# First norm of an encoder layer on one core: block 0 scaled per partition after its transposes, blocks 1 to 3 by rows, and the order of the start rewritten around it

## The chip, the core and the metric

The kernel runs on 1 core of one Trainium2 chip. The metric is the time of one execution in device microseconds. The kernel before has a median of 910.9 us over 3 runs (910.83 to 911.63). The engines are named as in the profile: PE is TensorE (its matmuls; PEld its weight loads), DVE is VectorE, ACT is ScalarE, POOL is GpSimd, SP is SyncE, which here issues most of the DMAs; ACTq and SPq are the queues from which ACT and SP issue DMAs.

## The reference, cut to what matters

One encoder layer on x of 512 tokens by 1024 features, f32. The change touches the first norm, the residual that is kept of it, and the first projections:

```
def layer_norm(x, g, b):
    mu = mean(x, -1); var = mean(square(x - mu), -1)
    return (x - mu) * rsqrt(var + 1e-5) * g + b

h = layer_norm(x, ln_in_g, ln_in_b)          # (512, 1024)
z = h @ w_in                                 # (512, 5376): q, k, v of two head groups
qa, ka, va, qb, kb, vb = split(z)            # rope on q and k, banded attention on both groups
...
h = layer_norm(ALPHA * h + mix, ln1_g, ln1_b)
```

Then come a cross attention over 256 memory rows and a convolutional gated feed-forward of width 2816, each with its own norm.

## The kernel before, in words

**Tiling.** The 512 tokens are four blocks of 128 rows. A matmul takes the normalised activations transposed (features on partitions, 8 tiles of 128, called k = 0 to 7), and each f32 operand as a sum of two fp32r parts, hi (a copy rounded by ACT) and lo (raw minus hi, by DVE). A product is then three matmuls for each k: hi by hi, lo by hi, hi by lo. So every weight tile costs one cast on ACT (line 136, or 278 and 423 in the first stage) and one subtraction on DVE (line 138, or 282 and 428).

**The first stage** (lines 374 to 520) is written out by hand. Within `manual_schedule` the order of PE, DVE and ACT instructions is the order of the code; other instructions (weight splits of the next stage) are put between them by the scheduler when the program is built. For each block b there are these steps:

- `stats(b)`: mean and variance on DVE (line 312), and rsqrt as a power on POOL (line 109).
- `gain(b)` (line 341): (x - mu) * g; `shift(b)` (line 348): times rsqrt plus bias. Both on DVE, two instructions of 128x512 each. Their g and b stand as rows on all partitions: PE spreads them with a matmul by ones (`ones_t`), the gain copied by ACT to SBUF (`gin`), the bias left in a PSUM tile (`bt`).
- `turn(b)` (line 355): 8 transposes on PE into the PSUM tiles t and o; `t_hi(b)` (ACT, line 362) and `t_lo(b)` (DVE, line 367) write the parts Thi and Tlo.
- `hh`, `lh`, `hl`: the 24 matmuls of block b that make v of the first dilated group (512 columns of w_in), summed in one PSUM bank, `vps[b]`.
- `spill(b)` (line 371): ACT scales h by ALPHA and stores it to DRAM, for the residual much later.

Matmuls by ones without a use, `busy(n)`, are put in at several places of PE's order.

**PSUM.** The tag g has two banks, handed out in turn; the tag s has two tiles of two banks. Before, the gain rows use both g banks, then `vps[0]` and `vps[1]` use them, and `vps[2]`, `vps[3]` are the two halves of an s tile. The next stage starts with the K projection and the Q projection (`chunk_fm`, line 602), each of 24 matmuls into a g bank, and so each waits until the g bank's last holder has been copied out.

**The copies of v.** ACT copies `vps[0]` and `vps[1]` to SBUF (line 497) ahead of block 3's matmuls in the code, and `vps[2]` and `vps[3]` (line 519) at the stage's end, behind the two sine activations (lines 515 and 517), which wait for a chain of DVE instructions on the positions (lines 507 to 516).

**Queues.** DMAs share eight completion semaphores in turn, and an issue waits until the semaphore's last DMA has landed. `raw` has three buffers: a weight's load is issued when the lo subtraction that read the buffer three loads earlier is done.

```
    def g_tile():
        return ps_tile("g", 2)
...
        vps = [g_tile(), g_tile()]
        two = s_tile()
        vps += [two[:, i, :] for i in range(2)]
...
        nc.scalar.activation(rsn, ang, AF.Sin, scale=cst[:, CS : CS + 1])
        nc.vector.scalar_tensor_tensor(kk, ang, -1.0, ang, ALU.mult, ALU.max)
        nc.scalar.activation(rc, kk, AF.Sin, scale=-1.0, bias=halfpi)
        for b in range(2, 4):
            nc.scalar.copy(vt[:, b, :], vps[b])
```

Of the kernel before, what the change touches and what calls it, by code (L numbers as in the profile page):

```python
# [9 lines left out]
F32 = mybir.dt.float32  # L10
# [7 lines left out]
P = 128  # L18
# [31 lines left out]

MEM_AT = (2, 0)
SEVEN = (5, 7, 9, 11, 13, 15, 17, 19)
WARM = (12, 3)
CI, CF, CS, CMA, CM1, CM3 = 0, 128, 129, 130, 514, 770
CW = 898

# [16 lines left out]
def hymba_layer(ctx: ExitStack, tc: tile.TileContext, A, cst_d, out):  # L73
# [121 lines left out]
    def ps_tile(tag, bufs, shape=None):  # L195
        return gpool.tile(shape or [P, 512], F32, tag=tag, bufs=bufs, name=tag)

    def g_tile():
        return ps_tile("g", 2)

    def s_tile():
        return ps_tile("s", 2, [P, 2, 512])
# [52 lines left out]
    gt = halves(gin)  # L255
    sbt = s_tile()
    bt = [sbt[:, n, :] for n in range(2)]
    wv0 = []

    def v_raw(i):  # L260
# [15 lines left out]
    def v_hi(i):  # L276
        for raw, hi, _ in v_parts(i):
            nc.scalar.copy(hi, raw)
# [13 lines left out]
    snk = cpool.tile([P, 8], F32, name="snk")  # L292
    nc.sync.dma_start(snk, A["attn_sink"].partition_broadcast(P)[:, 0, :])
    nsnk = cpool.tile([P, 8], F32, name="nsnk")
    cpool.tile([P, 40], F32, name="cfill")

    gwc, gdc = (p1.tile([P, 32], F32, name=n)[:, 0:NB] for n in ("gwc", "gdc"))
    gw4 = A["g_win"][0].rearrange("(s j d) -> s d j", s=2, d=HD)
# [10 lines left out]
    def stats(b):  # L309
        st = spool.tile([P, 2, 6], F32, tag="st", name="st")  # L310
        for i in range(2):
            nc.vector.bn_stats(st[:, i, :], h[b][:, i * 512 : (i + 1) * 512])  # L312
        mv, LN["rs", b] = moments(st)
        LN["mu", b] = mv[:, 0:1]
# [35 lines left out]
    def turn(b):  # L350
        LN["T", b] = []
        for i in range(2):
# [4 lines left out]
                )  # L357
            LN["T", b].append(ps.rearrange("p (k t) -> p k t", k=4))

    def t_hi(b):  # L360
        for i, src in enumerate(LN["T", b]):
            nc.scalar.copy(hT[0][:, 4 * i : 4 * i + 4, b * P : (b + 1) * P], src)
# [11 lines left out]
    with tc.manual_schedule(engines={nc.tensor.engine, nc.vector.engine, nc.scalar.engine}):  # L374
        for v, name in enumerate(("ln_in_g", "ln_in_b")):
            nc.scalar.dma_start(rows[0:1, v].rearrange("p n f -> p (n f)"), A[name].partition_broadcast(1))
        nc.scalar.dma_start(cst[:, 0:CMA], cst_d[:, 0:CMA])
        spare = ps_tile("t", 1)

        def busy(n, ps=None):  # L380
            for _ in range(n):
                mm((spare if ps is None else ps)[:, 0:P], ones_t, ones_t, True, True)

        busy(WARM[0])
        gps = [g_tile(), g_tile()]
        for n in range(2):
            mm(gps[n], ones_t, rows[:, 0, n, :], True, True)
            nc.scalar.copy(gt[n], gps[n])
        for n in range(2):
            mm(bt[n], ones_t, rows[:, 1, n, :], True, True)  # L390
        busy(WARM[1])
        vps = [g_tile(), g_tile()]
        two = s_tile()
        vps += [two[:, i, :] for i in range(2)]
        count = [0] * NB

        def v_mm(b, ks, a, w):
            for k in ks:
                mm(
                    vps[b], hT[a][:, k, b * P : (b + 1) * P], wv0[k // 2][1][w][:, k % 2, :],  # L400
                    count[b] == 0, count[b] == 3 * KD - 1,
                )
                count[b] += 1

        def hh(b, *ks):
            v_mm(b, ks, 0, 0)

        def lh(b, *ks):
            v_mm(b, ks, 1, 0)

        def hl(b, *ks):
            v_mm(b, ks, 0, 1)

        all_k = range(KD)
        first = {}

        def w_raw(n, c0):
            first[n] = [wpool.tile([P, KD, P], F32, tag="raw", bufs=3, name="raw")]
            nc.sync.dma_start(first[n][0], w_in.rearrange("(k p) f -> p k f", p=P)[:, :, c0 : c0 + P])

        def w_hi(n):
            first[n].append(wpool.tile([P, KD, P], F32R, tag="hi", bufs=6, name="hi"))
            nc.scalar.copy(first[n][1], first[n][0])

        def w_lo(n):
            raw, hi = first[n]
            lo = wpool.tile([P, KD, P], F32R, tag="lo", bufs=6, name="lo")
            nc.vector.tensor_tensor(lo, raw, hi.bitcast(F32), ALU.subtract)
            first[n] = (hi, lo)

        stats(0)
        gain(0)
        shift(0)
        v_hi(0)
        turn(0)
        t_hi(0)
        stats(1)
        t_lo(0)
        v_hi(1)
        busy(3, vps[1])  # L440
        hh(0, 0, 1)
        busy(2, vps[1])
        lh(0, 0, 1)
        v_hi(2)
        hh(0, 2, 3)
        lh(0, 2, 3)
        v_hi(3)
        gain(1)
        shift(1)
        hh(0, 4, 5)  # L450
        lh(0, 4, 5)
        hh(0, 6, 7)
        turn(1)
        t_hi(1)
        lh(0, 6, 7)
        stats(2)
        sums(3, 0)
        t_lo(1)
        v_lo(0)
        w_raw("k", KB)  # L460
        hh(1, *all_k)
        lh(1, *all_k)
        neg_mean(3)
        sums(3, 1)
        v_lo(1)
        w_raw("q", QB)
        for b in range(2):
            hl(b, 0, 1, 2, 3)
        gain(2)
        shift(2)  # L470
        spill(0)
        turn(2)
        t_hi(2)
        v_lo(2)
        for b in range(2):
            hl(b, 4, 5)
        hh(2, *all_k)
        gain(3)
        root(3)
        t_lo(2)  # L480
        lh(2, *all_k)
        w_hi("k")
        v_lo(3)
        spill(1)
        shift(3)
        hl(2, 0, 1, 2, 3, 4, 5)
        turn(3)
        t_hi(3)
        w_lo("k")
        t_lo(3)  # L490
        nc.vector.tensor_scalar_mul(nsnk, snk, -1.0)
        for b in range(3):
            hl(b, 6, 7)
        w_hi("q")
        w_lo("q")
        for b in range(2):
            nc.scalar.copy(vt[:, b, :], vps[b])
        hh(3, *all_k)
        lh(3, *all_k)
        hl(3, *all_k)  # L500
        spill(2)

        rc, rsn = rope
        posi = zs[:, 0, :].bitcast(I32)
        nc.sync.dma_start(posi, A["positions"].partition_broadcast(P)[:, 0, :])
        ang = zs[:, 2, :]
        nc.vector.tensor_copy(ang, posi)
        nc.vector.tensor_scalar_mul(ang, ang, cst[:, CF : CF + 1])
        kk = zs[:, 1, :]
        nc.vector.tensor_scalar(kk, ang, 1.0 / TWO_PI, MAGIC, ALU.mult, ALU.add)  # L510
        nc.vector.tensor_scalar_add(kk, kk, -MAGIC)
        for cc in (C1, C2, C3):
            nc.vector.scalar_tensor_tensor(ang, kk, -cc, ang, ALU.mult, ALU.add)
        nc.vector.tensor_scalar(ang, ang, PI_IN, -PI_IN, ALU.min, ALU.max)
        nc.scalar.activation(rsn, ang, AF.Sin, scale=cst[:, CS : CS + 1])
        nc.vector.scalar_tensor_tensor(kk, ang, -1.0, ang, ALU.mult, ALU.max)
        nc.scalar.activation(rc, kk, AF.Sin, scale=-1.0, bias=halfpi)
        for b in range(2, 4):
            nc.scalar.copy(vt[:, b, :], vps[b])
        spill(3)  # L520

    SWAP = [(i + 8 if i < 8 else i - 8 if i < 16 else i) for i in range(32)]
    rn = [0]
# [1036 lines left out]
```

## Time and profile before

| | |
|---|---|
| median of 3 runs | 910.9 us (910.83 to 911.63) |
| the profiled execution's own time | 911.27 us |
| its span, first to last instruction | 909.5 us |
| PE busy | 896.6 us, 99% of the span |
| DVE, ACT, POOL busy | 62%, 42%, 14% |
| first useful matmul of v | 13.10 us from the span's start |
| first matmul of the K projection | 40.16 us |

A row of the timeline reads: start in us, duration in us, engine, line, operation, written tile `<-` read tiles, shapes, xN for N merged instructions, and in brackets how long the engine was idle before it and what ended that. A plain f32 matmul stands as two rows. "PEclk" or the column behind an interval's length is the clock that TensorE was granted, as a share of full speed.

### The profile page before, as it was taken

Reading aid. Unit: us, or ns where it says so; the run is one execution under the profiler, and the core shown is the slowest. Engines: PE = TensorE matmul, PEld = TensorE weight load, DVE = VectorE, ACT = ScalarE, POOL = GpSimd, SP = SyncE. Lnnn points to the kernel's source line nnn. Section 1 sums busy time; section 2 is a strip of 40 time slices with the busy share of each in tenths; the row PEclk is TensorE's granted clock in tenths of the full one; section 3 lists DMA queues with packets and bytes.
Section 4 is the critical chain, followed back from the end, with each engine's and each line's share of the span. In section 5 each row is a group of like instructions: output and inputs, shape, how many; then the busy total and the mean of one; then the engine's idle time right before and its main releaser. Section 6 shows DMA issues by size and latency. Waiting matters only on the chain.

```text
span 909.5 us, 12905 instructions
## 1 busy us (share of the span) xinstructions
PE 896.6 (99%) x5097; PEld 768.3 (84%) x5097; DVE 560.2 (62%) x956; ACT 385.0 (42%) x672; POOL 127.2 (14%) x106
## 2 busy tenths in 40 slices
PE   9999999999999999999999999999999999999996
PEld 7778987898878798788988889799999999888885
DVE  7975146335446667869466576877777767433346
ACT  4563436415545576315454224344444345222210
POOL 1064033431443420010000010000000000000001
PEclk9999999999999999999999999999999999999999
DMA  6762041214221337316222304233333354223201
GB/s 220 225 213 70 24 139 47 73 67 117 70 70 47 93 117 233 138 46 171 85 70 70 93 25 129 82 93 93 95 114 94 96 160 140 93 93 103 83 23 70
DMA packets 116942, 92.84 MB, mean 102 GB/s; under 512 B 12472, under 2 KB 100752, under 8 KB 116882
## 3 DMA queue, kind: packets, MB, share of 16 engines
q1 hardware_dynamic: 116048, 89.80, 32.4%
q10 hardware_dynamic: 834, 2.22, 0.6%
q8 instruction: 40, 0.66, 0.3%
q14 instruction: 20, 0.16, 0.1%
HBM read 87.82 MB, written 4.19 MB: 101 GB/s over the span
## 4 chain that ended last, share of the span: by engine, by line
PE 95%; DVE 3%; ACT 1%; DMA 1%; issue 0%; POOL 0%; DVEq 0%; ACTq 0%
PE g L168 54%; PE s L168 24%; PE o L168 5%; PE t L168 4%; PE o L694 3%; PE s L682 2%; PE s L208 1%; DMA vt<-in_ln_in_g_dram 1%; PE s L1225 0%; DVE lo L282 0%; DVE oA L348 0%; DVE st L312 0%; DVE Tlo L367 0%; POOL zs L530 0%; DVE mx L1206 0%
## 5 line engine op out<-in xcount | busy, mean ns | idle before, releaser
L138 DVE TENSOR_TENSOR lo<-raw,hi 128x1024 fp32r<-128x1024 f32 x126 | 157.2, 1249 | 86.6 <-ACT hi L136 85.9
L136 ACT CAST hi<-raw 128x1024 fp32r<-128x1024 f32 x126 | 132.3, 1051 | 141.5 <-PE g L168 92.5
L168 PE MATMUL g<-Thi,hi 128*128 128x512 f32 x240 | 94.8, 395 | 0.0
L168 PE MATMUL g<-Tlo,hi 128*128 128x512 f32 x240 | 94.2, 393 | 0.0
L168 PE MATMUL g<-Thi,lo 128*128 128x512 f32 x240 | 94.0, 392 | 0.0
L109 POOL TENSOR_TENSOR rs<-ve,mhalf 128x1 f32<-128x1 f32 x18 | 15.3, 852 | 524.9 <-DVE ve L115 513.6
L530 POOL TENSOR_TENSOR zs<-zs,rsn 128x512 f32<-128x512 f32 x29 | 59.2, 2040 | 147.5 <-DVE zs L529 147.5
L168 PE MATMUL g<-Uhi,hi 128*128 128x512 f32 (+1 forms) x224 | 77.5, 346 | 1.0 <-ACT hi L136 1.0
L168 PE MATMUL g<-Ulo,hi 128*128 128x512 f32 (+1 forms) x224 | 77.1, 344 | 0.0
L168 PE MATMUL g<-Uhi,lo 128*128 128x512 f32 (+1 forms) x224 | 77.0, 344 | 0.0
L168 PE MATMUL g<-hi,Thi 128*128 128x512 f32 x184 | 71.6, 399 | 0.0
L168 PE MATMUL g<-hi,Tlo 128*128 128x512 f32 x184 | 70.9, 395 | 0.5 <-DVE Tlo L1173 0.5
L168 PE MATMUL g<-lo,Thi 128*128 128x512 f32 x184 | 70.7, 395 | 0.4 <-DVE lo L282 0.4
L528 DVE TENSOR_TENSOR zs<-g,rc 128x512 f32<-128x512 f32 x29 | 20.0, 689 | 68.2 <-PE g L168 31.6
L168 PE MATMUL g<-x,hi 128*128 128x256 f32 x320 | 58.8, 284 | 0.0
L168 PEld LDWEIGHTS g<-Thi,hi 128*128 128x128 f32 x240 | 45.1, 188 | 11.1 <-issue 0.9
L168 PEld LDWEIGHTS g<-Tlo,hi 128*128 128x128 f32 x240 | 45.1, 188 | 10.3 <-issue 1.4
L168 PEld LDWEIGHTS g<-Thi,lo 128*128 128x128 f32 x240 | 45.1, 188 | 9.3
L168 PEld LDWEIGHTS g<-x,hi 128*128 128x128 f32 x320 | 50.0, 192 | 0.5 <-issue 0.3
L168 PEld LDWEIGHTS g<-hi,Tlo 128*128 128x128 f32 x184 | 42.2, 230 | 6.4 <-DVE Tlo L1173 1.0
L168 PEld LDWEIGHTS g<-Uhi,hi 128*128 128x128 f32 x224 | 42.5, 190 | 5.8 <-ACT hi L136 1.2
L138 DVE TENSOR_TENSOR lo<-act,hi 128x512 fp32r<-128x512 f32 x22 | 14.8, 690 | 52.8 <-ACT hi L136 52.8
(363 smaller groups left out, 2091.8 us busy)
## 6 DMA issues: line engine op xcount, KB each, us to landing
raw<-in_w_in_dram SPq DMA_DIRECT2D x37, 512.0 KB, 3.8
raw<-in_w_gate_dram SPq DMA_DIRECT2D x22, 512.0 KB, 3.8
raw<-in_w_up_dram SPq DMA_DIRECT2D x22, 512.0 KB, 3.9
raw<-in_w_down_dram SPq DMA_DIRECT2D x22, 512.0 KB, 3.4
raw<-in_w_xk_dram SPq DMA_DIRECT2D x8, 512.0 KB, 3.9
raw<-in_w_xv_dram SPq DMA_DIRECT2D x8, 512.0 KB, 3.5
raw<-in_w_xq_dram SPq DMA_DIRECT2D x8, 512.0 KB, 4.6
raw<-in_w_xo_dram SPq DMA_DIRECT2D x8, 512.0 KB, 3.5
```

The lines of the kernel that those rows point to most:

```text
L109: nc.gpsimd.tensor_tensor(out_, in_, mhalf, ALU.pow)
L136: nc.scalar.copy(hi, raw)
L138: (eng or nc.vector).tensor_tensor(lo, raw, hi.bitcast(F32), ALU.subtract)
L168: on_pe(nc.tensor.matmul(o, l, r, start=first, stop=last))
L208: on_pe(nc.tensor.transpose(ps[:, i // 4, f : f + P], t[:, i * P : (i + 1) * P], ident))
L528: nc.vector.tensor_tensor(zc, ps, rc, ALU.mult)
L530: nc.gpsimd.tensor_tensor(sh, sh, rsn, ALU.mult)
L682: nc.tensor.transpose(tp[:, k, :], s_, ident)
L694: nc.tensor.matmul(o[HJ[j], t0:t1], lhs(j), rhs(j), start=i == 0, stop=i == len(parts) - 1)
```

## The change

- **Block 0** no longer has `gain` and `shift`. One DVE instruction (x - mu) * rs over 128x1024 normalises the rows; these are transposed; then, with features on partitions, g and b are one number per partition. `col_scale` applies them from PSUM into a new tile `fp0` (two tiles of k on ACT, six on DVE), and `col_hi` and `col_lo` make Thi and Tlo from it.
- The numbers per partition come as follows: two further DMAs on ACT's queue bring g and b as 8 rows of 128 each (`grow`), PE transposes the 16 rows, and DVE copies the result to `gcol`.
- **Block 0's residual** is made of the normalised rows by `resid`, four DVE instructions of 128x512 in two places, in place of `spill(0)` on ACT. The other spills move up by one place each.
- `stats(1)` and `v_hi(0)` go ahead of the gain rows; the bias rows go behind block 0's transposes; all `busy` matmuls but the first 12 are gone.
- `vps` changes places: blocks 0 and 1 now have the halves of the s tile, blocks 2 and 3 the two g banks.

The diff, with what only moves a constant left out:

```
-WARM = (12, 3)
+WARM = (12,)
...
+    fp0 = wpool.tile([P, KD, P], F32, tag="gb", bufs=2, name="fp0")
+    gcol = cpool.tile([P, 2 * KD], F32, name="gcol")
+    grow = zs[0 : 2 * KD, 1, 0:P]
...
+    def col_scale(ks, eng):
+        for k in ks:
+            g, o, src = gcol[:, k : k + 1], gcol[:, KD + k : KD + k + 1], LN["T", 0][k // 4][:, k % 4, :]
+            if eng is nc.scalar:
+                nc.scalar.activation(fp0[:, k, :], src, AF.Identity, scale=g, bias=o)
+            else:
+                nc.vector.tensor_scalar(fp0[:, k, :], src, g, o, ALU.mult, ALU.add)
+    def col_hi(k0, k1):
+        nc.scalar.copy(hT[0][:, k0:k1, 0:P], fp0[:, k0:k1, :])
+    def col_lo(k0, k1):
+        nc.vector.tensor_tensor(hT[1][:, k0:k1, 0:P], fp0[:, k0:k1, :], hT[0][:, k0:k1, 0:P].bitcast(F32), ALU.subtract)
+    def resid(part):
+        ah = oW[:, 0:2, :]
+        for i, z in enumerate(halves(h[0])):
+            if part == 0:
+                nc.vector.scalar_tensor_tensor(ah[:, i, :], z, ALPHA, gt[i], ALU.mult, ALU.mult)
+            else:
+                nc.vector.scalar_tensor_tensor(ah[:, i, :], bt[i], ALPHA, ah[:, i, :], ALU.mult, ALU.add)
+        if part == 1:
+            nc.scalar.dma_start(h_dram[0:P, :], ah.rearrange("p a f -> p (a f)"))
...
+        for v, name in enumerate(("ln_in_g", "ln_in_b")):
+            nc.scalar.dma_start(grow[v * KD : (v + 1) * KD, :], A[name].rearrange("(k p) -> k p", p=P))
...
         busy(WARM[0])
+        stats(0)
+        nc.vector.tensor_scalar(h[0], h[0], LN["mu", 0], LN["rs", 0], ALU.subtract, ALU.mult)
+        stats(1)
+        v_hi(0)
         gps = [g_tile(), g_tile()]
         for n in range(2):
             mm(gps[n], ones_t, rows[:, 0, n, :], True, True)
             nc.scalar.copy(gt[n], gps[n])
+        two = s_tile()
+        nc.tensor.transpose(two[:, 1, 0 : 2 * KD], grow, ident[0 : 2 * KD, 0 : 2 * KD])
+        nc.vector.tensor_copy(gcol, two[:, 1, 0 : 2 * KD])
+        turn(0)
         for n in range(2):
             mm(bt[n], ones_t, rows[:, 1, n, :], True, True)
-        busy(WARM[1])
-        vps = [g_tile(), g_tile()]
-        two = s_tile()
-        vps += [two[:, i, :] for i in range(2)]
+        vps = [two[:, i, :] for i in range(2)] + [g_tile(), g_tile()]
...
-        stats(0)
-        gain(0)
-        shift(0)
-        v_hi(0)
-        turn(0)
-        t_hi(0)
-        stats(1)
-        t_lo(0)
+        col_scale((0, 1), nc.scalar)
+        col_scale(range(2, KD), nc.vector)
+        col_hi(0, 2)
+        col_hi(2, 4)
+        col_lo(0, 4)
         v_hi(1)
-        busy(3, vps[1])
         hh(0, 0, 1)
-        busy(2, vps[1])
         lh(0, 0, 1)
+        col_hi(4, 8)
+        gain(1)
+        col_lo(4, 8)
...
-        spill(0)
+        spill(1)
...
-        spill(1)
+        spill(2)
...
+        resid(0)
         t_lo(3)
...
         w_lo("q")
+        resid(1)
         for b in range(2):
             nc.scalar.copy(vt[:, b, :], vps[b])
...
-        spill(2)
+        spill(3)
...
         for b in range(2, 4):
             nc.scalar.copy(vt[:, b, :], vps[b])
-        spill(3)
```

**How the order moves: PE at the start.** Before, from the first matmuls by ones (t) over the gain rows (g), the bias rows (s) and block 0's transposes (L355) on; the waits for semaphores stand in brackets (DMAHW is a DMA's, Pool, DVE and Activation an engine's).

```order
L168 MATMUL t<-zs 128x128 x11
L168 MATMUL g<-vt,zs 128x512 [waits DMAHW3_49,DVE_49]
L168 MATMUL g<-vt,zs 128x512
L168 MATMUL s<-vt,zs 128x512 [waits DMAHW5_49,Pool_49]
L168 MATMUL s<-vt,zs 128x512
L168 MATMUL t<-zs 128x128 x3
L355 MATMUL t<-cst,oA 128x128 [waits DMAHW0_49,DMAHW7_49,DVE_49,PE_49]
```

And PE at the start now (L425 is the transpose of the 16 rows of `grow`, L358 those of block 0):

```order
L168 MATMUL t<-zs 128x128 x11
L168 MATMUL g<-vt,zs 128x512 [waits DMAHW3_49,DVE_49]
L168 MATMUL g<-vt,zs 128x512
L425 MATMUL s<-cst,zs 128x16 [waits DMAHW7_49,DMAHW3_49,DMAHW1_49]
L358 MATMUL t<-cst,oA 128x128 [waits DVE_49,PE_49]
L358 MATMUL t<-cst,oA 128x128 x3
L358 MATMUL o<-cst,oA 128x128 x4
L168 MATMUL s<-vt,zs 128x512 [waits DMAHW5_49,Pool_49]
```

Ahead of block 0's transposes there now stands one that waits for three DMAs, and the bias rows have moved behind them.

**ACT at the head of its new DMAs.** What ACT's queue now holds there; the second pair brings `grow`.

```order
L405 DMA vt<-in_ln_in_g_dram 1x1024 [waits DVE_49]
L405 DMA vt<-in_ln_in_b_dram 1x1024 [waits Pool_49]
L406 DMA cst<-in_constants_dram 128x130
L408 DMA zs<-in_ln_in_g_dram 8x128 [waits DMAHW1_49]
L408 DMA zs<-in_ln_in_b_dram 8x128 [waits DMAHW3_49]
```

Before, only the first three stood there; the new two wait for DMAs that were issued earlier on the same semaphores (the first weight tile and the gain row).

**ACT at the end of the first stage.** Before, from the copies of `vps[0]` and `vps[1]` (g banks) on:

```order
L497 COPY vt<-g 128x512 x2
L371 ACTIVATE oW<-oB 128x1024
L136 CAST hi<-raw 128x1024
L372 DMA h_dram<-oW 128x1024
L136 CAST hi<-raw 128x1024 x3
L515 ACT_TABLE_LOAD
L515 ACTIVATE rsn<-zs,cst 128x512
L517 ACTIVATE rc<-zs,halfpi 128x512
L519 COPY vt<-s 128x512 x2
```

The same place now:

```order
L532 COPY vt<-s 128x512 x2
L400 ACTIVATE oW<-oB 128x1024
L136 CAST hi<-raw 128x1024
L401 DMA h_dram<-oW 128x1024
L136 CAST hi<-raw 128x1024
L550 ACT_TABLE_LOAD
L550 ACTIVATE rsn<-zs,cst 128x512
L552 ACTIVATE rc<-zs,halfpi 128x512
L554 COPY vt<-g 128x512 x2
```

The copies that free the g banks have gone from ahead of the casts and the sines to behind them; those that free an s tile have gone the other way.

**DVE at the same place, now,** from the lo part of the Q weights on (zs is the chain on the positions, L138 the lo parts of the next four weight tiles, L385 the second half of `resid`):

```order
L464 TENSOR_TENSOR lo<-raw,hi 128x1024
L385 SCALAR_TENSOR_TENSOR oW<-s,oW 128x512 x2
L542 CAST zs<-zs 128x512
L543 TENSOR_SCALAR zs<-zs,cst 128x512
L138 TENSOR_TENSOR lo<-raw,hi 128x1024
L545 TENSOR_SCALAR zs<-zs 128x512
L138 TENSOR_TENSOR lo<-raw,hi 128x1024
L546 TENSOR_SCALAR zs<-zs 128x512
L548 SCALAR_TENSOR_TENSOR zs<-zs 128x512
L138 TENSOR_TENSOR lo<-raw,hi 128x1024
L548 SCALAR_TENSOR_TENSOR zs<-zs 128x512 x2
L138 TENSOR_TENSOR lo<-raw,hi 128x1024
```

Before, five of the zs instructions stood ahead of the first L138; now two do, and the last one (L551, L516 before) stands behind all four of them, where before it stood behind three.

More of the change, by code (lines that the diff above doesn't have):

```diff
@@ L294, in hymba_layer @@
     nsnk = cpool.tile([P, 8], F32, name="nsnk")
-    cpool.tile([P, 40], F32, name="cfill")
+    cpool.tile([P, 24], F32, name="cfill")
     gwc, gdc = (p1.tile([P, 32], F32, name=n)[:, 0:NB] for n in ("gwc", "gdc"))
@@ L429, in w_lo @@
             first[n] = (hi, lo)
-        stats(0)
-        gain(0)
-        shift(0)
-        v_hi(0)
-        turn(0)
-        t_hi(0)
-        stats(1)
-        t_lo(0)
+        col_scale((0, 1), nc.scalar)
[3 more added lines that the diff above has]
+        col_lo(0, 4)
         v_hi(1)
-        busy(3, vps[1])
         hh(0, 0, 1)
-        busy(2, vps[1])
         lh(0, 0, 1)
-        v_hi(2)
+        col_hi(4, 8)
+        gain(1)
+        col_lo(4, 8)
         hh(0, 2, 3)
         lh(0, 2, 3)
-        v_hi(3)
-        gain(1)
-        shift(1)
+        v_hi(2)
         hh(0, 4, 5)
         lh(0, 4, 5)
+        v_hi(3)
+        shift(1)
         hh(0, 6, 7)
+        lh(0, 6, 7)
         turn(1)
         t_hi(1)
-        lh(0, 6, 7)
         stats(2)
```

## The prediction

> **What bounds the kernel now.** I read the page's busy table first, then PE's waits behind the first stage, then the timeline of all engines from 30 to 48 us.
>
> ```profile
> span 909.5 us, 12905 instructions
> ...
> PE 896.6 (99%) x5097; PEld 768.3 (84%) x5097; DVE 560.2 (62%) x956; ACT 385.0 (42%) x672; POOL 127.2 (14%) x106
> ```
>
> PE is busy 99% of the span, so whatever makes PE stand still is paid in full, unless PE had a later wait that shrinks by it. The waits of PE between 41 us and the end, all of them:
>
> ```profile
> PE g L168 <- ACT hi L136: 1.0, 1, 1.0
> PE g L168 <- DVE Tlo L1173: 0.5, 1, 0.5
> PE s L168 <- POOL x L531: 0.3, 1, 0.3
> PE s L682 <- ACT pu L774: 0.3, 1, 0.3
> ```
>
> They come to 2.1 us. So a delay of PE at 40 us can be given back by at most 2.1 us later; the rest arrives at the end. The question is when PE finishes v of the four blocks, and when it starts on the K projection. The timeline there:
>
> ```profile
> 31.38 1.22 DVE L428 TENSOR_TENSOR lo<-raw,hi 128x1024 fp32r<-128x1024 f32 x1
> 33.71 0.69 DVE L367 TENSOR_TENSOR Tlo<-t,Thi 128x512 fp32r<-128x512 f32 x1 [1.11 <-ACT Thi L362]
> ...
> 35.00 1.09 ACT L497 COPY vt<-g 128x512 f32<-128x512 f32 x2
> 35.15 1.23 DVE L428 TENSOR_TENSOR lo<-raw,hi 128x1024 fp32r<-128x1024 f32 x1
> 36.40 1.00 SPq L626 DMA_DIRECT2D raw<-in_w_in_dram  x2
> 38.35 1.98 PE L168 MATMUL s<-lo,Thi 128*128 128x512 f32 x8
> 39.06 1.23 DVE L138 TENSOR_TENSOR lo<-raw,hi 128x1024 fp32r<-128x1024 f32 x1 [0.17 <-PE s L168]
> 40.16 0.39 PE L168 MATMUL g<-Thi,hi 128*128 128x512 f32 x1
> 40.31 2.10 SPq L146 DMA_DIRECT2D raw<-in_w_in_dram  x2
> 42.22 1.05 ACT L136 CAST hi<-raw 128x1024 fp32r<-128x1024 f32 x1 [3.03 <-DMA raw<-in_w_in_dram]
> 44.25 1.05 ACT L136 CAST hi<-raw 128x1024 fp32r<-128x1024 f32 x1 [0.97 <-DMA raw<-in_w_in_dram]
> 47.24 0.71 ACT L517 ACTIVATE rc<-zs,halfpi 128x512 f32<-128x512 f32 x1
> 47.86 1.05 ACT L519 COPY vt<-s 128x512 f32<-128x512 f32 x2
> ```
>
> The last eight matmuls of v (38.35) run at 1.81 / 8 = 0.226 us each, and K's first matmul (40.16) follows without a gap. Its g bank was block 0's; ACT had copied that out at 35.00. Blocks 2 and 3, in an s tile, are copied out only at 47.86: ACT first waits for two weight tiles (42.22 and 44.25, idle 3.03 and 0.97 ahead of them) and runs the sines. Before, nobody needs that s tile by then.
>
> **The change, first term: the K projection behind the sines.** Now blocks 2 and 3 hold the g banks, so K's first matmul needs the copy that stands behind the sines, and Q's the one after it. Nothing that waits on PE's order can fill the hole: PE takes its instructions in order. With the old times alone, K would start when the first of the two copies (1.05 / 2) is done, at 48.4: 8.2 us late.
>
> It comes later still, since DVE's work around it grows. I need DVE's short operations on the positions:
>
> ```profile
> 37.27 0.43 DVE L510 TENSOR_SCALAR zs<-zs 128x512 f32<-128x512 f32 x1
> ...
> 38.19 0.69 DVE L513 SCALAR_TENSOR_TENSOR zs<-zs 128x512 f32<-128x512 f32 x1
> ```
>
> `resid` adds four operations of the second kind: at a little under 0.69 each, 1.31 in each of its two places (of the pair at 14.71, below, the last ends after 1.41). The first stands behind the lo part of K's weights; DVE is idle 1.11 us there (row 33.71), so it costs what follows only 0.2 to 0.3, or all 1.31 if that idle time is used up by DVE's own delay. Let all of v be 0.6 us late (second term). Then t_lo(3) runs from about 34.5, the lo part of Q's weights ends at 37.1 (36.38 before), and the second half of `resid` and the first two operations on the positions end at 39.35. The first L138 needs PE's second pair among the last eight, 0.7 behind their start as before (39.06 to 38.35): 39.65 to 40.85.
>
> Two DMAs hang on this, by the three raw buffers. The one behind Q's lo part took 42.22 - 36.38 = 5.84 until ACT began on it: 42.95 now, and its cast ends at 44.0. The one behind the first L138 took 44.25 - 40.31 = 3.94: 44.8, cast until 45.85. DVE takes the third L138 44.05 to 45.2 (1.15 from start to start), two operations of 0.66 until 46.5, the fourth L138 until 47.65, then 0.45 and 0.69 for the last two of the positions: 48.75. The cosine takes 0.71, the copy another 0.57: K starts at about 50.1. That is 9.95 us late in all, 0.6 of it v's delay, so PE stands about 9.3 us. The shortest hole is the old time, 8.2 less the 0.2 between; the longest adds both halves of `resid` in full to it, 8.2 + 2.6 = 10.8.
>
> **Second term: the start.** Rows of the chain of waits and of the timeline:
>
> ```profile
> 1.96 4.69 DMA vt<-in_ln_in_g_dram
> 4.41 1.66 SPq L268 DMA_DIRECT2D raw<-in_w_in_dram  x2
> 8.58 1.88 PE L168 MATMUL s<-vt,zs 128*128 128x512 f32 x4
> 11.41 0.63 PE L355 MATMUL t<-cst,oA 128*128 128x128 f32 x4 [0.28 <-PE t L168]
> 13.10 0.71 PE L168 MATMUL g<-hi,Thi 128*128 128x512 f32 x2
> 14.71 1.41 DVE L341 SCALAR_TENSOR_TENSOR oA<-oA,mv,gin 128x512 f32<-128x512 f32 x2
> 17.34 1.28 DVE L312 BATCH_NORM_STATS2 st<-oB 128x6 f32<-128x512 f32 x2
> 59.10 0.29 DVE L725 CUSTOM_DVE_ANT_0 pu<-s,cst 128x128 f32<-128x128 f32 x1
> 59.43 0.40 ACT L728 ACTIVATE pu<-pu,stT 128x128 f32<-128x128 f32 x1 [0.63 <-DVE stT L725]
> ```
>
> The change takes away `gain(0)` and `shift(0)` and lets the statistics of blocks 0 and 1 run in idle time of DVE, but all of block 0 now waits for the two small DMAs of `grow`. ACT can't issue the second one before the gain row has landed: 1.96 + 4.69 = 6.65. (The first waits for the first weight tile, for which SP's second issue of line 268, ended at 6.07, waited too.) No row shows a DMA of 8 rows of 512 bytes on ACT's queue in this traffic. The nearest is the gain row itself, 4.69 from issue to landing; the ends are the fastest and the slowest medians of the DMA table that come into question:
>
> ```profile
> out_dram<-h SPq DMA_DIRECT2D x8, 256.0 KB, 2.1
> ...
> cst<-in_constants_dram ACTq DMA_DIRECT2D x1, 65.0 KB, 5.5
> ```
>
> I take 4.69: landed at 11.35 (8.75 to 12.15). The Trainium skill, page "DMA: Bandwidth & Descriptors", section "Anatomy of one DMA — SWDGE (gpsimd) path", gives a DMA about 2.0 us of fixed cost plus its bytes over 436 GB/s. By that rule `grow` would be there at about 8.7; the gain row's 4.69 for 4 KB speaks against it in this traffic.
>
> Behind the landing: transpose and `gcol` until 11.8; block 0's transposes 11.5 to 12.6 (0.63 for four); two scales on ACT (0.40, the second 0.3 later) until 12.7; six on DVE at 0.2 to 0.29 until 14.1; col_lo 0.6; `gain(1)` 1.31, col_lo 0.6, `shift(1)` 1.31. So stats(2) starts at 17.95, against 17.34: 0.6 late (2.0 early to 1.4 late with the bounds). From there DVE's list is the old one, and so v ends 0.6 late. PE's own start, 12.6 + 1.7 for the bias rows (8.58) = 14.3 against 13.10, is hidden behind DVE. ACT's table load and `v_hi(0)` come later too, but the gain rows are needed by DVE only at 14.7: nothing. The loads of x's blocks 2 and 3 are issued one landing later, 1.3 us; stats(2) has that to spare.
>
> **Third term: the clock.** The first matmuls, the same kind when warm, and the end of the span, with the granted clock third from the end in the last two rows:
>
> ```profile
> 0.99 4.97 PE L168 MATMUL t<-zs 128*128 128x128 f32 x24 [0.99 <-POOL zs L247]
> 12.52 0.83 PE L168 MATMUL g<-zs 128*128 128x128 f32 x6
> 901.57 0.39 PE L168 MATMUL g<-hi,lo 128*128 128x512 f32 x1
> 902.00:906.00 4.00, 0.00 (x0) 0.00 (x0) 3.90 (x8) 0.00 (x0) 0.92 (x1) 1.00 0.00 0
> 906.00:909.50 3.50, 0.00 (x0) 0.00 (x0) 0.48 (x1) 0.00 (x0) 0.00 (x0) 0.55 0.40 150
> ```
>
> After the last matmul (ended 901.96) the clock stays full past 906 and is about half from then on: some 4 us of standing still take it away. At the start, 24 matmuls took 0.207 each where later six took at most 0.14: half speed for 4 to 5 us of work. A hole of 9.3 us is over the 4 us, so K starts at half speed. For 4.5 us it does 10 matmuls in place of 20; 10 x 0.226 = 2.2 us lost (0 if the clock stays, 2.5 if it takes 4.97). The Trainium skill, page "TensorE: Matmul & The Clock Gate", section "What's actually happening", says the clock falls to half after an idle window of about 3.4 us and comes back after a busy one. By that figure the term would be 1.7 and the time 922.3; the trace agrees on the half.
>
> **Sum.** 9.95 for K's start, 2.2 for the clock, less 0.3 for the later wait on POOL, whose chain no longer starts late: 11.85 us. On the profiled execution's 911.27 (its span 909.5 and 1.77 around it) that is 923.1; on the median of 910.9, 0.4 lower, 922.8.
>
> **Rivals.**
> - `grow` lands early, at about 8.75: v ends 2.0 early in place of 0.6 late, the hole stays: 922.8 - 2.6 = 920.2. For it: 4 KB is little. Against: the gain row, as small, took 4.69. It is also what the Trainium skill's DMA page would give.
> - The clock isn't lost in the hole: 920.6. Against it stands the end of the span.
> - The clock is lost at the start as well. PE would stand from 8.6 to 11.4, 2.8 us, which is under 4; if `grow` comes at 12.15 it is 3.6. Then block 0's transposes, the bias rows and the first eight or so matmuls run at half, some 2.5 us more on top of 0.8: 926.
> - Not slower: K's bank is free earlier, because K's first matmul waits for the copy of block 0, not of block 2. Place: the two copies of v. Price: the hole of 9.3 and the clock's 2.2 go, 922.8 - 11.5 = 911.3, and with an early `grow` 908.7. It decides as soon as that copy ends before v does (40.9). The code hands out the two g banks in turn, and the last two holders are blocks 2 and 3, so this would need another bank for K than I read.
>
> **How the numbers follow.** Forecast 0.62; early `grow` 0.14; clock kept 0.07; clock lost twice 0.13; bank free 0.04, half of it with an early `grow`. About 0.2%, 1.8 us, is what a measurement can tell from no change; only the last rival gets within it (0.02) or below it (0.02), so slower has 0.96. The range goes from 919.0 (early `grow` with the shortest hole, 8.0 of 9.3) to 926.0 (clock lost twice).
>
> **What would show it.** In the changed kernel's profile: a wait of PE for ACT's copy at line 554, 8 to 11 us long, ahead of the first g<-Thi,hi; rows of K's first ten matmuls about 0.45 apart; a granted clock near half in those microseconds; the copy of vt<-g behind the cosine at about 50; L425 on PE at about 11.4. Wrong would be: K without a gap behind v, or a hole under 6 us, or PE's later waits shrinking by more than 2.

## The result and the profile after

The changed kernel takes 923.71 us (923.35 to 925.34, 4 runs), against 911.0 (910.83 to 911.63): 1.0141 times as long, 95% interval 1.0129 to 1.0153, or 12.7 us more. The profiled execution is the longest of the four, 925.34; the other three had spans of 921.5 to 922.0, so some 1.6 of what its rows add up to isn't in the median.

The page's busy table, and the waits of PE from 41 us to the end (total, times, longest), of the changed kernel:

```profile
span 923.5 us, 12890 instructions
...
PE 899.0 (97%) x5082; PEld 768.4 (83%) x5082; DVE 562.0 (61%) x964; ACT 385.1 (42%) x674; POOL 125.9 (14%) x106
```

```profile
PE g L168 <- ACT vt L554: 9.2, 1, 9.2
PE g L168 <- ACT hi L136: 1.0, 1, 1.0
PE s L716 <- ACT pu L808: 0.9, 2, 0.6
PE g L168 <- DVE Tlo L1207: 0.5, 1, 0.5
```

One wait is new, and it is the one that the first step named: the K projection waits for ACT's copy of block 2's bank. The later ones are those of before, but that POOL's 0.3 is gone and ACT's 0.3 for `pu` is 0.9. The timeline around the hole:

```profile
39.85 1.98 PE L168 MATMUL g<-lo,Thi 128*128 128x512 f32 x8
...
46.35 1.04 ACT L136 CAST hi<-raw 128x1024 fp32r<-128x1024 f32 x1 [2.81 <-DMA raw<-in_w_in_dram]
...
49.81 0.72 ACT L552 ACTIVATE rc<-zs,halfpi 128x512 f32<-128x512 f32 x1
50.44 1.05 ACT L554 COPY vt<-g 128x512 f32<-128x512 f32 x2
51.06 0.80 PE L168 MATMUL g<-Thi,hi 128*128 128x512 f32 x1 [9.23 <-ACT vt L554]
...
55.49 0.40 PE L168 MATMUL g<-Tlo,hi 128*128 128x512 f32 x1
```

The last eight matmuls of v start 1.5 later than before (38.35), PE stands 9.23, and K starts at 51.06, 10.9 late. Its first ten matmuls start 0.44 apart on average ((55.49 - 51.06) / 10); behind 55.49 it is 0.23 to 0.24. The same stretches by interval; the column behind POOL's is the granted clock:

```profile
8.60:10.90 2.30, 0.00 (x0) 0.00 (x0) 0.69 (x3) 1.51 (x3) 0.55 (x1) 1.00 1.14 392
11.10:12.90 1.80, 1.80 (x10) 1.80 (x10) 0.17 (x1) 0.66 (x2) 0.00 (x0) 0.51 0.88 310
13.00:14.50 1.50, 1.50 (x3) 0.52 (x2) 1.42 (x5) 1.11 (x4) 0.00 (x0) 0.50 1.00 372
...
41.90:45.20 3.30, 0.00 (x0) 0.00 (x0) 3.27 (x5) 1.65 (x2) 0.00 (x0) 1.00 0.83 257
45.30:51.00 5.70, 0.00 (x0) 0.00 (x0) 3.70 (x6) 4.24 (x6) 0.00 (x0) 0.50 0.97 316
51.10:55.50 4.40, 4.40 (x11) 3.43 (x12) 0.00 (x0) 0.39 (x1) 0.00 (x0) 0.50 0.14 54
```

The clock falls to half twice. The second time is the one that was forecast: PE stands from about 41.8, the clock is full until 45.2 and half until 55.5. The first time was not: PE stood only 2.4 us (8.55 to 10.96) and from 11.1 to 14.5 has half the clock. What that does to the start:

```profile
6.49 0.28 ACTq L408 DMA_DIRECT2D zs<-in_ln_in_b_dram  x1
...
10.96 0.20 PE L425 MATMUL s<-cst,zs 16*128 16x16 f32 x1 [2.41 <-DMA zs<-in_ln_in_b_dram]
11.10 1.11 PE L358 MATMUL t<-cst,oA 128*128 128x128 f32 x4
12.00 1.06 PE L358 MATMUL o<-cst,oA 128*128 128x128 f32 x4
...
13.08 0.73 DVE L370 TENSOR_SCALAR fp<-t,gcol 128x128 f32<-128x128 f32 x2 [1.71 <-PE o L358]
...
18.85 1.28 DVE L315 BATCH_NORM_STATS2 st<-oB 128x6 f32<-128x512 f32 x2
```

The short rows land 4.4 us after their issue (6.49 to 10.87 in the chain of waits). Then block 0's transposes take 1.1 for four instead of 0.63, and block 2's statistics start at 18.85, 1.5 later than before.

### The profile page after: what moved, and what is told of

Its sections match the earlier page's. It is cut to its first block, busy times and chain, and to the rows that moved or that the text cites. A ratio compares the mean times of both kernels' runs of the same rounds, so it can differ in the third digit from the quotient of the medians.

```text
span 923.5 us, 12890 instructions
## 1 busy us (share of the span) xinstructions
PE 899.0 (97%) x5082; PEld 768.4 (83%) x5082; DVE 562.0 (61%) x964; ACT 385.1 (42%) x674; POOL 125.9 (14%) x106
## 4 chain that ended last, share of the span: by engine, by line
PE 89%; DVE 4%; DMA 4%; ACT 2%; issue 1%; SPq 0%; DVEq 0%; ACTq 0%
PE g L168 52%; PE s L168 21%; PE o L168 5%; PE t L168 4%; PE o L728 3%; PE s L716 2%; DMA raw<-in_w_mix_out_dram 2%; DMA raw<-in_w_in_dram 1%; PE s L208 1%; DVE lo L138 1%; ACT hi L136 1%; ACT pu L808 1%; DMA vt<-in_ln_in_g_dram 0%; DMA zs<-in_ln_in_b_dram 0%; PE s L1259 0%
## 5 line engine op out<-in xcount | busy, mean ns | idle before, releaser
L138 DVE TENSOR_TENSOR lo<-raw,hi 128x1024 fp32r<-128x1024 f32 x126 | 156.9, 1247 | 91.2 <-ACT hi L136 90.2
L168 PEld LDWEIGHTS g<-hi,Thi 128*128 128x128 f32 x184 | 42.4, 230 | 5.8 <-DVE h L1158 0.5
```

What stands on the lines that cost most here:

```text
L138: (eng or nc.vector).tensor_tensor(lo, raw, hi.bitcast(F32), ALU.subtract)
L168: on_pe(nc.tensor.matmul(o, l, r, start=first, stop=last))
```

## The experiments

The theory: the swap of v's banks puts K behind the sines, PE stands some 9 us for it, and the clock is lost there; the rest is the start. The rival: the loss comes from the start and from VectorE's longer list, and the bank only shows it. "Before" was 911.1 to 911.2 us in each set of runs.

**1. The banks back.** One line of the changed kernel:

```
-        vps = [two[:, i, :] for i in range(2)] + [g_tile(), g_tile()]
+        vps = [g_tile(), g_tile()] + [two[:, i, :] for i in range(2)]
```

> The changed kernel with one line put back: blocks 0 and 1 hold the g banks again, blocks 2 and 3 the halves of the s tile. Theory (the hole of 9.2 us is the wait for the copies behind the sines, and the half clock of 2.2 us comes from the hole): K's first matmul follows v without a gap at about 41.8 us, the granted clock is full there, and 11.4 of the 12.7 us go. What stays is the start (v 1.5 us late) and, since the cosine now comes at about 50 in place of 47.9, a wait of PE for POOL of some 2 us at the first scores: about 914. Rival (the loss is made by the start and by VectorE's longer list, and the hole only stands where PE would have waited anyway): PE waits 8 to 10 us at another place soon after, the time stays at 921 to 924.

916.67 us (915.06 to 918.34), ratio 1.0062, 1.0046 to 1.0079. The hole is gone and 7.0 us with it. About 914 had been expected, but PE now meets waits that it didn't have before. PE's waits behind 41 us, and ACT's timeline, of this run:

```profile
PE g L168 <- DVE zs L563: 1.9, 1, 1.9
PE s L168 <- POOL x L565: 0.6, 1, 0.6
```

```profile
49.36 1.05 ACT L136 CAST hi<-raw 128x1024 fp32r<-128x1024 f32 x1 [1.86 <-DMA raw<-in_w_in_dram]
...
52.35 0.71 ACT L552 ACTIVATE rc<-zs,halfpi 128x512 f32<-128x512 f32 x1
```

The third chunk of 24 matmuls behind v (the first is K's) takes the bank that the rope of the first must have left, and that rope waits for the cosine, at 52.35 instead of 47.24 before. The chain of waits shows why it is so late: the weight tile whose cast stands ahead of the sines (49.36 above) is loaded only when VectorE's list has freed a buffer, and that transfer takes from 43.16 to 49.28. So behind the hole lay a second delay.

**2. The copies ahead.** The banks as changed, but blocks 0, 1 and 2 are copied out where blocks 0 and 1 were, and block 3 ahead of the sines:

```
-        for b in range(2):
+        for b in range(3):
             nc.scalar.copy(vt[:, b, :], vps[b])
...
         hl(3, *all_k)
+        nc.scalar.copy(vt[:, 3, :], vps[3])
...
-        for b in range(2, 4):
-            nc.scalar.copy(vt[:, b, :], vps[b])
```

> The changed kernel with its banks as they are, but the copies of blocks 2 and 3 ahead of the sines on ScalarE: block 2 with blocks 0 and 1, block 3 right behind its last matmul. Theory: it's the place of the copies and not the bank as such; K waits at most 1 us, for block 2's copy behind the two others, and the clock stays full: about 915. Rival (the tag of the bank itself costs, or the start does): 921 to 924.

915.04 us (914.71 to 916.41), ratio 1.0047, 1.0032 to 1.0062. It isn't the banks as such but the place of the copy: K waits 0.4 for it. The cosine's lateness shows here too (1.1 for `zs`, 0.5 for POOL).

**3. The swap alone**, in the kernel before:

```
-        vps = [g_tile(), g_tile()]
         two = s_tile()
-        vps += [two[:, i, :] for i in range(2)]
+        vps = [two[:, i, :] for i in range(2)] + [g_tile(), g_tile()]
```

> The kernel before with the swap of banks alone: blocks 0 and 1 in the s tile, 2 and 3 in the g banks; all else as before, no column scale, no further DMAs. Theory: PE waits 8.2 us ahead of K (40.2 to 48.4), K's first ten matmuls run at half clock (2.2 us): 911 + 10.1 = about 921. Rival (the start and VectorE's list): 911 to 912.

922.27 us (920.97 to 922.75), ratio 1.0125, 1.0109 to 1.0142. Nothing else of the change is in it, and it makes 11.1 of the 12.7 us. Its timeline and its clock:

```profile
47.71 0.80 PE L168 MATMUL g<-Thi,hi 128*128 128x512 f32 x1 [8.09 <-ACT vt L518]
```

```profile
40.00:42.50 2.50, 0.00 (x0) 0.00 (x0) 2.08 (x4) 1.05 (x1) 0.00 (x0) 1.00 0.85 238
42.50:47.50 5.00, 0.00 (x0) 0.00 (x0) 3.27 (x4) 3.97 (x5) 0.00 (x0) 0.50 0.85 225
47.80:52.30 4.50, 4.50 (x11) 3.54 (x12) 0.00 (x0) 1.30 (x2) 0.00 (x0) 0.50 0.57 219
```

The hole is 8.1 without VectorE's additions and 9.2 with them. So the rival falls as the account of the 12.7. What it names still costs 5.5 once the banks are back (run 1); the two costs overlap, since 11.1 and 5.5 are more than 12.7.

**4. The clock held.** The changed kernel with 40 matmuls that nobody reads, between v and K:

```
         hl(3, *all_k)
+        idle = ps_tile("t", 1)
+        for _ in range(40):
+            mm(idle[:, 0:P], ident, ident, True, True)
```

> The changed kernel with 40 matmuls without a use (identity by identity, 128 columns, some 8.6 us of PE time) between v and K, inside the hole. Theory: the hole stays as long as it was (K starts at about 51), but the clock stays full, and the 2.2 us that K lost go: about 921.5. Rival (K's slow start is hidden by the weights' splits or given back later): 923 to 924, as without them.

922.15 us (921.25 to 923.0), ratio 1.0122, 1.0107 to 1.0137; 1.6 under the changed kernel, and the two ranges don't touch. The clock is full through the hole and behind it:

```profile
41.90:52.00 10.10, 9.01 (x81) 8.82 (x79) 7.22 (x11) 6.00 (x7) 0.00 (x0) 1.00 0.87 280
52.30:56.30 4.00, 4.00 (x18) 3.31 (x19) 0.00 (x0) 0.35 (x1) 0.00 (x0) 1.00 0.14 53
```

K starts at 52.22, 1.2 after the changed kernel's. The 40 matmuls aren't the reason, for PE stands another 1.3 behind them and waits for ACT's copy: by the chain of waits, the weight transfer ahead of the sines took 5.46 here and 4.46 there. K's eleventh matmul starts at 54.61 all the same, the changed kernel's at 55.49. So the clock is a term of its own, of about 2 us (1.2 and 0.9).

**5. Block 0's residual off VectorE.** What is left with the banks back, 5.5 us, has two candidates: the start, and `resid`. This run, on top of run 1, takes `resid` out and puts `spill(0)` to `spill(3)` back to their places; gain and bias are then missing from block 0's residual:

```
-        resid(0)
-        resid(1)
...
+        spill(0)
```

> The changed kernel with the four banks of v as before (the run with the banks back, 916.7 us), and block 0's residual written as before, by one ScalarE copy and its write at the old place; it leaves gain and bias out of block 0's residual, so that part of the output differs. Theory (what is left of the loss with the banks back is 1.4 us of late v and about 2 us that VectorE's two residual steps, 1.29 us each, and the casts put ahead of the sines add): 912.5 us, 911.8 to 913.5, K no later at its fourth chunk than v is. Rival (all of it comes from the start, VectorE's later steps are covered): 915.5 to 917.

912.6 us (912.04 to 914.05, 11 runs), ratio 1.0015, 1.0007 to 1.0024. As the theory has it: 4.1 us less than with `resid` (in the profiles 0.5 of it is v, which ends earlier here: K starts at 41.07, in run 1 at 41.53). The cosine is at 48.18, and PE's waits behind 41 us are those of before. This run also shows the start with the clock kept: PE stood 2.2 us for the same rows.

```profile
10.90:12.90 2.00, 2.00 (x12) 1.50 (x12) 0.61 (x3) 1.21 (x3) 0.00 (x0) 1.00 0.89 317
```

```profile
10.80 0.20 PE L425 MATMUL s<-cst,zs 16*128 16x16 f32 x1 [2.20 <-DMA zs<-in_ln_in_b_dram]
10.93 0.66 PE L358 MATMUL t<-cst,oA 128*128 128x128 f32 x4
...
12.47 0.73 DVE L370 TENSOR_SCALAR fp<-t,gcol 128x128 f32<-128x128 f32 x2 [1.26 <-ACT fp L368]
...
18.24 1.27 DVE L315 BATCH_NORM_STATS2 st<-oB 128x6 f32<-128x512 f32 x2
```

From L425 to VectorE's first scaling it is 1.67 here and 2.12 in the changed kernel: the clock at the start costs 0.45 in that execution.

**6. Unread matmuls at the start**, 15, on top of run 1:

```
             nc.scalar.copy(gt[n], gps[n])
+        busy(15)
         two = s_tile()
```

> Banks as before, and 15 matmuls that nobody reads, of 128 columns, ahead of the transpose of the two short rows, so that PE does not stand before it. Theory (2.4 us of standing cost the clock for 3.4 us, and the slow transposes and bias rows made v later): full clock at the transposes, 0.66 and 0.66 us instead of 1.11 and 1.06 in the changed kernel, bias rows 1.9 us instead of 2.7, v 0.4 to 0.9 us earlier, 915.9 us, 915.3 to 916.4. Rival (v is set by VectorE's chain from the landing of the rows on, and PE's clock lies beside it): no gain, 916.5 to 917.

918.03 us (916.62 to 919.5), ratio 1.0071, 1.0057 to 1.0084: no gain. They were too many. They took 3.51 us and pushed the transposes back:

```profile
8.54 3.51 PE L168 MATMUL t<-zs 128*128 128x128 f32 x30
11.98 0.23 PE L426 MATMUL s<-cst,zs 16*128 16x16 f32 x1
...
56.60 0.80 PE L168 MATMUL g<-Thi,hi 128*128 128x512 f32 x1 [3.33 <-DVE zs L564]
```

The clock was full at the transposes, but they came 1.0 later than in run 1. For that the wait for the rope grew from 1.9 to 3.3, and there the clock was lost (half from 56.0 to 62.8). This is the slowest of the five executions. About the clock at the start this run says nothing; how steeply a late start is paid behind v, it does.

**7. The short rows first**, on top of run 1. The long rows' matmuls stand behind block 0's first four of v, and 9 unread ones in their old place:

```
         for v, name in enumerate(("ln_in_g", "ln_in_b")):
-            nc.scalar.dma_start(rows[0:1, v].rearrange("p n f -> p (n f)"), A[name].partition_broadcast(1))
+            nc.scalar.dma_start(grow[v * KD : (v + 1) * KD, :], A[name].rearrange("(k p) -> k p", p=P))
         nc.scalar.dma_start(cst[:, 0:CMA], cst_d[:, 0:CMA])
         for v, name in enumerate(("ln_in_g", "ln_in_b")):
-            nc.scalar.dma_start(grow[v * KD : (v + 1) * KD, :], A[name].rearrange("(k p) -> k p", p=P))
+            nc.scalar.dma_start(rows[0:1, v].rearrange("p n f -> p (n f)"), A[name].partition_broadcast(1))
...
```

> Banks as before; the two short rows of gain and bias are issued first on ScalarE's queue, the constants third as before, the long rows last, and the four matmuls on the long rows stand behind block 0's first four v matmuls, with 9 unread matmuls in their old place. Theory (the start is late since the short rows land at 10.9 us): they land near 7, the transposes start near 8.5 instead of 11.1, VectorE's scaling near 9.7 instead of 13.1, v up to 1.5 us earlier, 915.3 us, 914.3 to 916.2. Rival (weights and x blocks bound v, or the long rows' matmuls take the gain back): 916.5 to 918.

919.24 us (919.0 to 921.35), ratio 1.0092, 1.0078 to 1.0106. The rival was right: the transposes do start at 8.57, but then the long rows' matmuls stand in v's way, the second pair waiting for ScalarE to empty its bank; the fifth of v's matmuls starts at 19.22, in run 1 at 16.39. Not all of that need be the long rows': behind two gaps of 1.47 us the clock was half from 13.2 to 16.6, and the two shares aren't separated.

```profile
14.36 1.91 PE L168 MATMUL g<-vt,zs 128*128 128x512 f32 x2
16.94 1.13 PE L168 MATMUL g<-vt,zs 128*128 128x512 f32 x2 [0.68 <-ACT gin L473]
...
19.22 1.03 PE L168 MATMUL g<-hi,Thi 128*128 128x512 f32 x2
```

**8. Run 6 with half of `resid` early**, behind the copy of `gcol`. Block 2's spill then overwrites that half, so block 0's residual in the output differs:

```
         nc.vector.tensor_copy(gcol, two[:, 1, 0 : 2 * KD])
+        resid(0)
...
-        resid(0)
```

> The 15 unread matmuls, and the first of VectorE's two residual steps moved to the start, behind the copy of the gains, where VectorE waits for block 0's transposes anyway. Theory: beside the run with the unread matmuls alone, 1.3 us less on VectorE between v and K and one cast fewer ahead of the sines, so 1 to 2 us off it: 914.5 us, 913.8 to 915.4. Rival (VectorE's residual steps are covered): as the run with the unread matmuls alone, 915.5 to 917.

916.79 us (914.36 to 917.89), ratio 1.0056, 1.0043 to 1.0070: 1.2 less than run 6, above the range that I had given and in the rival's, since run 6 had been too high. The direction fits: the wait for the rope shrank from 3.3 to 1.2. It isn't shown, though: the intervals overlap, and the traces are of run 6's slowest and of run 8's fastest execution.

**9. The short rows first, the long ones in gaps**, on top of run 5, with the DMAs in the order of run 7; the gain's copies and `col_lo(4, 8)` then stand ahead of `gain(1)`:

```
-        for n in range(2):
-            mm(gps[n], ones_t, rows[:, 0, n, :], True, True)
-            nc.scalar.copy(gt[n], gps[n])
+        busy(7)
...
         turn(0)
+        gps = [two[:, n, :] for n in range(2)]
         for n in range(2):
-            mm(bt[n], ones_t, rows[:, 1, n, :], True, True)
+            mm(gps[n], ones_t, rows[:, 0, n, :], True, True)
...
         hh(0, 0, 1)
+        mm(bt[0], ones_t, rows[:, 1, 0, :], True, True)
         lh(0, 0, 1)
+        mm(bt[1], ones_t, rows[:, 1, 1, :], True, True)
```

> The run with the banks back and block 0's residual on ScalarE (912.6 us; it leaves gain and bias out of block 0's residual, and so does this one), and the two short rows issued first. The long rows' gains now stand behind block 0's transposes and go to the free pair of banks, the two bias matmuls stand behind block 0's first two and next two v matmuls, so that none of them holds v for more than 1 us. Theory (the start is late since the short rows land at 10.9): transposes near 8.6 instead of 10.9, the scaling near 10.7 instead of 12.5, block 2's statistics 1 to 1.8 us earlier than 18.2, v 0.5 to 1.5 us earlier, 911.6 us, 910.9 to 912.3. Rival (v's weights or the long rows bound the start): 912.4 to 914.

910.67 us (910.27 to 911.52, 11 runs), ratio 0.9994, 0.9985 to 1.0004: the time of before. The rows are there before PE has finished its unread matmuls:

```profile
0.73 0.58 ACTq L405 DMA_DIRECT2D zs<-in_ln_in_g_dram  x1
...
7.37 0.23 PE L423 MATMUL s<-cst,zs 16*128 16x16 f32 x1
7.88 0.63 PE L358 MATMUL t<-cst,oA 128*128 128x128 f32 x4 [0.28 <-DVE oA L417]
...
16.32 1.28 DVE L315 BATCH_NORM_STATS2 st<-oB 128x6 f32<-128x512 f32 x2
```

Statistics 1.9 earlier than in run 5, time 1.9 less. Runs 1, 5 and 9 take the loss back in three steps, of 7.0, 4.1 and 1.9 us; but runs 5 and 9 leave gain and bias out of block 0's residual, and so aren't the whole computation.

**10. A complete residual on GpSimd**, on top of run 1: ScalarE copies the bias rows, GpSimd multiplies and adds, ScalarE scales.

```
+            nc.gpsimd.tensor_tensor(z, z, gt[i], ALU.mult)
...
+            nc.gpsimd.tensor_tensor(ah[:, i, :], z, ah[:, i, :], ALU.add)
...
+            nc.scalar.activation(oW[:, i, :], bt[i], AF.Copy)
...
+        nc.scalar.activation(oW[:, 0:2, :], oW[:, 0:2, :], AF.Copy, scale=ALPHA)
```

> Banks back, and block 0's residual with its gain and bias complete, but off VectorE: ScalarE copies the bias rows (two copies of 512 columns), GpSimd multiplies and adds (four steps of 128x512), ScalarE scales and writes it behind block 1's. Theory (VectorE's two residual steps are what makes the sines late): as the run that left gain and bias out, 912.6 us, plus what ScalarE's extra copies cost: 913.2 us, 912.3 to 914.2. Rival (GpSimd's four steps, some 5 us, hold back a norm's root or ScalarE's copy, or the lateness comes from the start): 915 to 917.

913.04 us (912.55 to 914.01, 11 runs), ratio 1.0021, 1.0012 to 1.0030. With the whole of the computation in it, 3.6 us under run 1: VectorE's share is shown without leaving anything out.

**11. Runs 9 and 10 together.**

> Both: the residual on GpSimd and the short rows first, the long rows' matmuls as in the first run of this set. Theory: the two gains add, 912.2 us, 911.2 to 913.2, level with the kernel before. Rival (GpSimd or the long rows take it back): 914 to 917.

912.39 us (912.14 to 913.47, 11 runs), ratio 1.0014, 1.0005 to 1.0023. That is inside the range of the theory, but the gains don't add in full: the early rows, worth 1.9 in run 9, are worth 0.65 here against run 10. GpSimd's product falls on VectorE's `gain(1)`, which takes 2.1 more than in run 10, and block 2's statistics start at 18.45, 2.1 later than in run 9. In this execution the clock was half from 20.7 to 24.1 as well; its share isn't separated.

```profile
13.66 3.00 POOL L382 TENSOR_TENSOR oA<-oA,gin 128x512 f32<-128x512 f32 x2 [3.61 <-ACT gin L475]
13.74 3.47 DVE L344 SCALAR_TENSOR_TENSOR oA<-oA,mv,gin 128x512 f32<-128x512 f32 x2
```

It is the best complete version of the change that was run, and still 1.2 slower than before.

**12. Run 6 with 8 unread matmuls**, which end before the rows land:

```
+        busy(8)
```

> The run with the banks back (916.7 us, 915.1 to 918.3) and 8 unread matmuls, 1.9 us of PE by the 0.117 us a pass that the 15 too many took, in front of the transpose of the short rows, so that PE stands only some 0.4 us there and the transposes are not pushed back. Theory (the clock is lost at the start in some executions, and that is part of the late v and of the spread): full clock at the transposes in the profile, 0.66 us each, every time near the lower end, median 915.2 us, 914.6 to 915.9, spread under 1.5 us. Rival (the spread is that of the weight transfers ahead of the sines, and the clock at the start costs nothing): median 916.2 to 917.5, spread about 3 us as before.

915.17 us (914.32 to 919.06), ratio 1.0054, 1.0039 to 1.0069. The transposes run at full clock:

```profile
11.16 0.66 PE L358 MATMUL t<-cst,oA 128*128 128x128 f32 x4
```

The median is the theory's, the spread, 4.7 us, is the rival's, and the interval overlaps run 1's. What the clock at the start is worth isn't settled by times; run 5's rows (0.45) are the best measure, for a fall as early as the changed kernel's. In run 1's trace the clock fell at 11.7, behind the first four transposes, and block 2's statistics started at 18.43, no later than here (18.47).

## Why the prediction was right, step by step

- **The hole: right.** 9.3 was forecast and 9.23 measured; runs 1 to 3 show its cause. K's start came at 51.06 and not at 50.1, because v was later than I had put it. That the lengths agree to 0.1 is partly luck. I had VectorE's list as the last link, with 3.94 for the weight transfer behind its first L138; in the trace that transfer is the link (41.81 to 46.27, 4.46), and VectorE stands 0.65 for the cast behind it. In run 4 it took 5.46, and K started 1.2 later.
- **The clock in the hole: right.** 2.2 was forecast; K's delay grows from 10.9 to 13.1 by its eleventh matmul (55.49 against 42.43 before), 2.2, and run 4 gives 1.6 back in spite of a start of K 1.2 later. The 4.5 us of half clock that I had taken from the start of the span came to 4.4 here (51.06 to 55.51), to 5.1 in run 3 and to 6.2 in run 6, so the exact size was luck; nor does the trace call that start half, where the granted clock reads 1.00.
- **The start: right in kind, wrong in size**, and the term that makes the difference: 0.6 was forecast, v was 1.5 late. The landing was taken at 11.35 and was 10.87, which helped by 0.5. Two parts of the chain behind it were too short. I had VectorE's six scalings end at 14.1, 1.4 us after 12.7; they took 1.92 (13.08 to 15.00, where the next operation starts; as in run 5), 0.5 more. And the transposes were at half clock, 0.45 by run 5. And even at full clock the first scaling came 1.67 behind L425, where I had 1.3, 0.4 more. Together 0.85 of the 0.9. The rule for a DMA that the prediction set beside its 4.69, from the Trainium skill, page "DMA: Bandwidth & Descriptors", section "Anatomy of one DMA — SWDGE (gpsimd) path", is a fit for DMAs that GpSimd issues; these rows came by ACT's queue, and took 4.4.
- **"Some 4 us of standing still take it away": wrong**, the step that failed. I read it off the end of the span, and gave the loss at the start 0.13 because 2.8 us of standing "is under 4". 2.4 us were enough there, and 2.2 in runs 2 and 4, while 2.2 in runs 5 and 10 left the clock alone. The time from PE's last matmul to the half clock was 2.6 at the start, 3.4 in the hole, 2.9 in run 3, 2.1 in run 4 and 4.4 at the end of the kernel before (901.96 to 906.38): no fixed length of standing. The rival with this name had 2.5 us "on top" of the start, and the measured cost is 0.45, because it only delays PE's chain to VectorE and the bias rows lie beside VectorE's work.
- **POOL's wait, less 0.3: right**, but ACT's wait for `pu` grew by 0.6 in the profiled execution.
- **The sum.** Forecast 11.85. By the rows it is 1.5 for v, 9.4 for the hole (the 9.23, and 0.17 by which K before started ahead of the modelled end of v's last matmul) and 2.2 for the clock, less 0.4 that is given back by 70 us, POOL's 0.3 among it: 12.7, which is the difference of the medians. The profiled execution's span is 14.0 longer. Its rows stand 12.7 behind until 200 us, 0.9 more by 234 and 0.5 more by 388, both times with a weight transfer in the chain of waits. The other three executions have spans 1.5 to 2.0 shorter; where they are faster no trace shows.
- **A rival that would have come out wrong.** "K's bank is free earlier" was priced at 911.3. Runs 1 and 2 are that case, at 916.7 and 915.0. I had charged `resid` to the hole alone (0.2 to 2.6 of its length). But the cosine waits behind the same VectorE list, and without the hole its lateness is paid at the third chunk behind v.

What stays open: why run 1 and run 12 spread over 3 to 5 us where runs 9 to 11 spread over 1.3 to 1.5. PE's wait of some 2 us for the rope, which the latter lack, is a likely place. In the traces of runs 2, 1 and 6 the transfer ahead of the sines took 6.0, 6.1 and 7.5, and PE waited 1.1, 1.9 and 3.3 behind it; in run 6 that took the clock. The mean granted clock of each execution fits in part: in run 12 it was 0.998 in the three fastest (914.3 to 914.7) and 0.995 in the two slowest (916.3 and 919.1), but in run 8, from 914.4 to 917.9, it was 0.997 to 0.999. Only one execution of each run has a trace, so this stays open.

## What to carry to other kernels

Look for who frees the bank of the next stage's first matmul, and where that copy stands in its engine's order: a swap of one line cost 11 us here, and neither a busy share nor the diff's arithmetic shows it. When such a hole is closed, ask what it covered, since the late cosine cost 4 us more only after that. A new small transfer at the start of the critical path should be issued ahead of the large ones, and the work that it displaces must go into gaps, or the gain is lost again (run 7 against run 9, though in run 7 the clock was lost too).

## What the runs showed of the hardware

**The clock.** The length of one gap doesn't decide. At the start the clock fell after 2.18 us of standing (run 2), 2.22 (run 4), 2.33 (run 1) and 2.41 (the changed kernel), and stayed full after 2.20 (run 5) and 2.25 (run 10). In run 11 it fell at 20.7, behind gaps of only 0.5 and 0.9. Run 2 first, then run 10:

```profile
10.95 0.20 PE L425 MATMUL s<-cst,zs 16*128 16x16 f32 x1 [2.18 <-DMA zs<-in_ln_in_b_dram]
...
11.90:15.30 3.40, 3.40 (x8) 1.53 (x6) 2.68 (x8) 3.01 (x7) 0.00 (x0) 0.50 0.96 293
```

```profile
10.63 0.20 PE L422 MATMUL s<-cst,zs 16*128 16x16 f32 x1 [2.25 <-DMA zs<-in_ln_in_b_dram]
...
10.70:12.60 1.90, 1.90 (x12) 1.39 (x13) 0.47 (x2) 1.11 (x3) 1.03 (x1) 1.00 0.93 337
```

In run 2 PE was busy again for a microsecond when the clock fell. What the falls and returns have in common is their distance. In the changed kernel they come at 11.14, 14.55, 45.27 and 55.51, which is 1, 9 and 3 times 3.41 us apart; the half clock lasted 3.41 in runs 1, 2, 4, 7 and 11 as well, twice that in run 6 and three times that in run 3. So in each trace the clock changes only on a grid of 3.41 us. That the grid's place against the gap decides whether the gap costs the clock is the reading that fits equal gaps with unequal outcomes; what share of a stretch PE must stand for it the runs don't settle. The Trainium skill, page "TensorE: Matmul & The Clock Gate", section "What's actually happening", has a free-running window of about 3.4 us that decides: that fits this grid. Its "idle window" ahead of the fall can't be one without any matmul, since in the 3.41 us ahead of 11.14 PE stood for 2.41.

**GpSimd beside VectorE.** In run 11 VectorE's two multiplications, with two operands from SBUF, took 3.47 beside GpSimd's product; in run 10, where that product (11.57 to 14.08) fell on the scalings that read PSUM, these took what they take without it (1.36 for four in the changed kernel as well):

```profile
11.57 2.51 POOL L382 TENSOR_TENSOR oA<-oA,gin 128x512 f32<-128x512 f32 x2 [1.64 <-PE t L358]
```

```profile
12.95 1.36 DVE L370 TENSOR_SCALAR fp<-o,gcol 128x128 f32<-128x128 f32 x4
14.82 1.41 DVE L344 SCALAR_TENSOR_TENSOR oA<-oA,mv,gin 128x512 f32<-128x512 f32 x2
```

The Trainium skill, page "GPSIMD Engine Reference", section "1. Specifications", names this contention for VectorE instructions with two SBUF inputs; the runs agree, with 3.47 against 1.41.
